# Column-group products of the modulation vectors, issued as groups of four

## The chip, the cores and the metric

One core of a Trainium2 chip runs the whole program as one launch. The time is device microseconds of that launch. Engines are named as in the profile: PE is TensorE (matrix products), PEld its weight loads, DVE is VectorE, ACT is ScalarE, POOL is GpSimd, SP is the queue from which nearly all DMAs are issued. Each engine works through its instructions in the order in which the scheduler of the language has put them; that order is fixed when the program is built.

## The reference

Two layers over 1024 latent and 256 context tokens of width 1024. In every layer six modulation vectors (shift, scale and gate of two sub-layers) are computed from the conditioning vector `c` and, for the context tokens, from `c_ctx`:

```python
c_act, cc_act = silu(c), silu(c_ctx)
for l in range(2):
    mx = c_act @ w_mod[l] + b_mod[l]        # 1024 x 6144, split into sh1, sc1, gt1, sh2, sc2, gt2
    mc = cc_act @ w_mod[l] + b_mod[l]
    hx = rmsnorm(x, g_pre_mix[l]) * (1 + sc1) + sh1
    yx, yc = ab_mixer(hx, hc, ...) if l == 0 else na_mixer(hx, hc, ...)
    x = x + gt1 * rmsnorm(yx, g_post_mix[l])
    fx = rmsnorm(x, g_pre_ffn[l]) * (1 + sc2) + sh2
    x = x + gt2 * rmsnorm(swiglu(fx, ...), g_post_ffn[l])
```

Layer 0's mixer is an RG-LRU block beside a 2-D Fourier transform, layer 1's is a neighbourhood attention; the context stream goes through the same sub-layers in layer 0.

## The kernel before, in words

The big matrix products split each float32 operand into two halves and take three products of 128 x 128 by 128 x 512 for one (`mm3`, lines 362 to 364). The modulation vectors are a different, thin sort of product: 2 rows (c and c_ctx, in `self.sil`, padded to 32 columns) against 1024 x 6144 float32 weights. One tile of weights is 128 rows by 512 columns, 256 KB, loaded to a buffer named `mraw`. Its product has an output of 32 x 512, and so four of them fit beside each other in one PSUM tile of 128 x 512: product j goes to partitions 32j to 32j+31 with `tile_position=(0, 32 * j)`, the j-th group of 32 columns of the array. [...] I call products that stand next to each other in PE's order, with no other work between, a **run**.

The vectors come in groups g of 2048 columns, and in three manners:

- Layer 0, g = 0, in quarters of 512 columns at the start of the program (`quarter` in `mixer`, lines 571 to 600). Step r of a quarter loads four tiles (rows 128k, k = 4r to 4r+3, line 583; a ring of 10 buffers) and issues their products (line 584); product j of a step takes row tile 4r + j. Quarter q+1 is issued between the first projections' products (`early_mm`).
- Layer 0, g = 1 and 2, in `mod_steps` (lines 419 to 435): 16 steps of four tiles (line 416) and four products (line 430), one for each column group j. The ring `mraw` has 3 buffers here (`open_mraw()`, line 670). `fill()` puts 12 of the steps between the LRU's parts, and the last four stand in the Fourier part (`for f in mods: f()`). The bias (line 478) and a gain (line 499) pass through the same ring.
- Layer 1, in `mod_steps_dve` (lines 437 to 474): DVE multiplies each tile by the column `sil[:, k, w]` and adds it up into `acc` (lines 452 and 454), and one product with a column of ones (line 460, `sum_up`) sums each `acc` over its partitions. g = 0 has two rows (c and c_ctx) and is done in layer 0's FFN, first half (`ffn_up`). g = 1 and 2 have one row, `acc` is a ring of 2, and they are fillers in the first block of `ffn_down`: after 8 loads of a column group j comes its sum. That block multiplies 22 tiles of hidden units by each half of w_down's columns; at the change of halves DVE takes the first half's sums from PSUM (`PostNorm.done`, line 257).

After the last product of a group `mod_row` adds the bias (DVE, line 480), and `mod_finish` turns the row into columns (PE, line 487).

Of the kernel before, what the change touches and what calls it, by code (L numbers as in the profile page):

```python
# [8 lines left out]
F32 = mybir.dt.float32  # L9
# [7 lines left out]
P = 128  # L17
# [4 lines left out]
KD = D // P  # L22
# [259 lines left out]
class Kernel:  # L282
# [130 lines left out]
    def mod_load(self, l, g, k, j):  # L413
# [2 lines left out]
        self.nc.sync.dma_start(out=raw, in_=self.a["w_mod"][l, k * P:(k + 1) * P, c:c + 512])  # L416
        return raw

    def mod_steps(self, l, g, pp, tag):

        nc = self.nc
        st = {}

        def step(k):
            if k == 0:
                st["ps"] = self.t(pp, [P, 512], F32, tag)
            ps = st["ps"]
            for j in range(4):
                raw = self.mod_load(l, g, k, j)
                nc.tensor.matmul(ps[32 * j:32 * j + 32, :], self.sil[:, k, :], raw, start=(k == 0), stop=(k == KD - 1),  # L430
                                 tile_position=(0, 32 * j))
            if k == KD - 1:
                self.mod_finish(l, g, self.mod_row(l, g, ps), pp, tag)

        return [lambda k=k: step(k) for k in range(KD)]

    def mod_steps_dve(self, l, g, pp, tag, rows):


        nc = self.nc  # L440
        st = {"acc": {}}

        def add_up(j, ks):
            for k in ks:
                raw = self.mod_load(l, g, k, j)
                for w in rows:
                    if k == 0:
                        st["acc"][j, w] = self.t(self.mraw, [P, 512], F32, "acc", bufs=2)
                    acc = st["acc"][j, w]
                    s = self.sil[:, k, w:w + 1]  # L450
                    if k == 0:
                        nc.vector.tensor_scalar(acc, raw, s, None, op0=ALU.mult)
                    else:
                        nc.vector.scalar_tensor_tensor(acc, raw, s, acc, op0=ALU.mult, op1=ALU.add)

        def sum_up(j):
            if j == 0:
                st["ps"] = self.t(pp, [P, 512], F32, tag)
            for w in rows:
                nc.tensor.matmul(st["ps"][32 * j:32 * j + 32, :], self.ones[:, w, :], st["acc"][j, w], start=(w == rows[0]),  # L460
                                 stop=(w == rows[-1]), tile_position=(0, 32 * j))

        def step(j, h):
            if h == 0 and j > 0:
                sum_up(j - 1)
            add_up(j, range(4 * h, 4 * h + 4))

        def last():
            sum_up(3)
            st["mr"] = self.mod_row(l, g, st["ps"])  # L470

        return ([lambda j=j, h=h: step(j, h) for j in range(4) for h in range(2)]
                + [last, lambda: self.mod_finish(l, g, st["mr"], pp, tag)])
# [63 lines left out]
    def mixer(self):  # L537
        nc, tc, a = self.nc, self.tc, self.a
# [31 lines left out]
        def quarter(q):  # L570

            st = {}

            def step(r):
                if r == 0:
                    st["ps"] = self.t(z0p, [P, 512], F32, "m", bufs=2)
                    b = st["b"] = self.t(self.mraw, [P, 512], F32, "mraw")
                    nc.sync.dma_start(out=b, in_=a["bmod0"][:, q, :])
                for j in range(4):
                    k = 4 * r + j  # L580
                    raw = self.t(mrp, [P, 512], F32, "mraw")
                    src = a["w_mod"][0, k * P:(k + 1) * P, 0:2048].rearrange("p (v c) -> p v c", v=2)
                    nc.sync.dma_start(out=raw.rearrange("p (v c) -> p v c", v=2), in_=src[:, :, 256 * q:256 * q + 256])
                    nc.tensor.matmul(st["ps"][32 * j:32 * j + 32, :], self.sil[:, k, :], raw, start=(r == 0), stop=(r == 1),
                                     tile_position=(0, 32 * j))

            def finish():
                mr = self.t(sp, [P, 512], F32, "mq")
                nc.vector.tensor_tensor(mr, st["ps"], st["b"], op=ALU.add)
                pt = self.t(tp, [P, 4, P], F32, "t")  # L590
                for i in range(4):
                    nc.tensor.matmul(pt[:, i, :], mr[:, i * P:(i + 1) * P], self.sel[:, :, 0:64], start=True, stop=True)
                src = pt.rearrange("p (v i) (w r) -> p v i w r", v=2, w=2)
                c = slice(2 * q, 2 * q + 2)
                for w in range(2):
                    nc.vector.tensor_copy(self.mt[0][:, 0:2, w, c], src[:, :, :, w, 0])
                    nc.vector.scalar_tensor_tensor(self.G[0][0][:, w, c], self.mt[0][:, 1, w, c], 1.0, self.gpre[:, 0, 0, c],
                                                   op0=ALU.add, op1=ALU.mult)

            return [lambda: step(0), lambda: step(1), finish]  # L600
# [66 lines left out]
        self.ystack = ExitStack()  # L667
        rxp = self.pool("rx", side="left", stack=self.ystack)
        xtp = self.pool("xt", bufs=4, side="left", stack=self.ystack)
        self.open_mraw()  # L670
        tstack = ExitStack()
        lp = self.pool("lru", bufs=2, side="left", stack=tstack)
        ep = self.pool("lrup", side="left", stack=tstack)
# [1384 lines left out]
```

## Time and profile before

| | us |
|---|---|
| three timed runs | 2745.85, 2751.33, 2755.67; median 2751.33 |
| profiled execution, its own time | 2753.36 |
| span of it, first to last instruction | 2751.6 |

The mean granted clock of PE over the span is 0.978 of full speed. The views used below are the page (busy times of the engines), windows (the same for stretches of the span, with PE's granted clock and the DMA engines' share), the timelines of single engines (start, length and name of instructions in order; "[1.81 <-DMA x]" is idle time just before and what ended it), and the lists of waits (who waited for whom: total us, times, longest). The start of the span is 0.

### The profile page before, as it was taken

Reading aid. Unit: us, or ns where it says so; the run is one execution under the profiler, and the core shown is the slowest. Engines: PE = TensorE matmul, PEld = TensorE weight load, DVE = VectorE, ACT = ScalarE, POOL = GpSimd, SP = SyncE. Lnnn points to the kernel's source line nnn. Section 1 sums busy time; section 2 is a strip of 40 time slices with the busy share of each in tenths; the row PEclk is TensorE's granted clock in tenths of the full one; section 3 lists DMA queues with packets and bytes.
Section 4 is the critical chain, followed back from the end, with each engine's and each line's share of the span. In section 5 each row is a group of like instructions: output and inputs, shape, how many; then the busy total and the mean of one; then the engine's idle time right before and its main releaser. Section 6 shows DMA issues by size and latency. Waiting matters only on the chain. (4 is left out here: it accounts for less than half of the span.)

```text
span 2751.6 us, 36277 instructions
## 1 busy us (share of the span) xinstructions
PE 2603.5 (95%) x12770; PEld 2120.1 (77%) x12770; DVE 1716.0 (62%) x2576; ACT 1257.5 (46%) x2245; POOL 990.2 (36%) x868
## 2 busy tenths in 40 slices
PE   7999999899999999999978999999997999999997
PEld 3677577688888887777866787899875888888786
DVE  3765275866543435666567655788677666656966
ACT  3676255422222323334553333899754333333443
POOL 1000013544343441002036333788536554542811
PEclk9999999899999999999998999999999999999999
DMA  7333463233222126876535545878541333235534
GB/s 246 107 113 124 127 205 139 73 104 102 89 70 73 65 72 219 303 235 241 192 122 181 179 172 177 198 185 190 145 148 54 103 112 115 87 109 179 208 100 145
DMA packets 187815, 399.59 MB, mean 145 GB/s; under 512 B 19697, under 2 KB 50033, under 8 KB 185586
## 3 DMA queue, kind: packets, MB, share of 16 engines
q1 hardware_dynamic: 187634, 397.28, 44.9%
q8 instruction: 101, 1.65, 0.3%
q14 instruction: 80, 0.66, 0.1%
HBM read 311.75 MB, written 85.46 MB: 144 GB/s over the span
## 5 line engine op out<-in xcount | busy, mean ns | idle before, releaser
L362 PE MATMUL d<-u,u 128*128 128x512 f32 x768 | 305.9, 401 | 20.1 <-ACT u L328 10.7
L363 PE MATMUL d<-u,u 128*128 128x512 f32 x768 | 306.5, 399 | 11.3 <-DVE u L329 11.2
L364 PE MATMUL d<-u,u 128*128 128x512 f32 x768 | 305.0, 397 | 0.1
L328 ACT ACTIVATE u<-r 128x512 fp32r<-128x512 f32 x249 | 154.8, 628 | 246.2 <-DVE u L329 53.8
L329 DVE TENSOR_TENSOR s<-r,s 128x512 fp32r<-128x512 f32 x208 | 166.2, 805 | 158.5 <-ACT s L328 157.6
L262 POOL TENSOR_TENSOR ss<-ss 128x1 f32<-128x1 f32 x36 | 12.8, 356 | 672.0 <-ACT junk L260 671.9
L363 PE MATMUL g<-u,s 128*128 128x512 f32 x624 | 245.4, 394 | 5.2 <-POOL u L174 4.3
L362 PE MATMUL g<-u,s 128*128 128x512 f32 x624 | 244.6, 393 | 3.7 <-ACT u L124 1.9
L329 DVE TENSOR_TENSOR u<-r,u 128x512 fp32r<-128x512 f32 x249 | 190.9, 773 | 87.1 <-ACT u L328 83.9
L364 PE MATMUL g<-u,s 128*128 128x512 f32 x624 | 244.6, 392 | 0.0
L328 ACT ACTIVATE s<-r 128x512 fp32r<-128x512 f32 x208 | 127.5, 629 | 247.6 <-PE g L364 149.8
L200 POOL TENSOR_TENSOR r<-rg,ru 128x512 f32<-128x512 f32 x52 | 73.1, 1405 | 406.2 <-DMA rg<-in_w_gu_dram 140.6
L362 PEld LDWEIGHTS d<-u,u 128*128 128x128 f32 x768 | 147.2, 192 | 62.8 <-ACT u L328 18.2
L363 PEld LDWEIGHTS d<-u,u 128*128 128x128 f32 x768 | 147.3, 192 | 44.7 <-DVE u L329 15.4
L1651 POOL TENSOR_TENSOR s<-s,sm 128x640 f32<-128x640 f32 (+1 forms) x128 | 151.0, 1200 | 59.3 <-DVE sm L1647 51.0
L364 PEld LDWEIGHTS d<-u,u 128*128 128x128 f32 x768 | 147.6, 192 | 32.0 <-DVE u L329 1.2
L362 PE MATMUL d<-u,ga 128*128 128x512 f32 x416 | 164.4, 395 | 2.6 <-ACT ga L328 2.5
L364 PE MATMUL d<-u,ga 128*128 128x512 f32 x416 | 163.3, 393 | 0.7 <-DVE ga L329 0.6
L363 PE MATMUL d<-u,ga 128*128 128x512 f32 x416 | 163.2, 392 | 0.0
L1183 POOL TENSOR_TENSOR ub<-ub,ua 128x512 f32<-128x512 f32 x44 | 72.4, 1645 | 205.0 <-DVE ua L1182 198.0
L363 PEld LDWEIGHTS g<-u,s 128*128 128x128 f32 x624 | 118.2, 190 | 30.8 <-POOL u L174 5.5
L362 PEld LDWEIGHTS g<-u,s 128*128 128x128 f32 x624 | 118.1, 189 | 30.1 <-ACT u L124 3.5
(445 smaller groups left out, 6972.2 us busy)
## 6 DMA issues: line engine op xcount, KB each, us to landing
mraw<-in_w_mod_dram SPq DMA_DIRECT2D x192, 256.0 KB, 3.8
rg<-in_w_gu_dram SPq DMA_DIRECT2D x44, 512.0 KB, 4.3
ru<-in_w_gu_dram SPq DMA_DIRECT2D x44, 512.0 KB, 3.8
r<-in_w_down_dram SPq DMA_DIRECT2D x88, 256.0 KB, 4.1
u<-hd SPq DMA_DIRECT2D x44, 512.0 KB, 5.2
x<-x SPq DMA_DIRECT2D x40, 512.0 KB, 4.9
qd<-qd SPq DMA_DIRECT2D x32, 512.0 KB, 10.6
r<-in_w_qkv_dram SPq DMA_DIRECT2D x52, 256.0 KB, 3.1
```

The source lines that it names most:

```text
L200: pool(rs[3], rg[:, h1], ru[:, h1], op=ALU.subtract)
L262: nc.gpsimd.tensor_tensor(st, ss[:, 0:1], ss[:, 1:2], op=ALU.add)
L328: i = nc.scalar.activation(hi, src, AF.Copy) if eng == "act" else nc.vector.tensor_copy(hi, src)
L329: j = nc.vector.tensor_tensor(lo, src, hi.bitcast(F32), op=ALU.subtract)
L362: nc.tensor.matmul(ps, lhs[0], rhs[0], start=start, stop=False)
L363: nc.tensor.matmul(ps, lhs[0], rhs[1], start=False, stop=False)
L364: nc.tensor.matmul(ps, lhs[1], rhs[0], start=False, stop=stop)
L1183: pool(ub, ub, ua, op=add)
L1651: pin(nc.gpsimd.tensor_tensor(s, s, sm.to_broadcast([P, nl + L]), op=ALU.mult))
```

## The change

1. A new helper `four` issues the four products of a step in one piece, j = 3 first, then 0, 1, 2, and pins them in PE's order (`keep_in_program_order`). `mod_steps` and the quarters use it; all four loads of a step are issued first.
2. In layer 1, for the groups with one row, the four sums over partitions are issued together by `four` after the fourth column group, and `acc` becomes a ring of 4.
3. The ring `mraw` of the mixer grows from 3 to 5 buffers.

```diff
--- before.py
+++ after.py
@@ -416,6 +416,13 @@
         self.nc.sync.dma_start(out=raw, in_=self.a["w_mod"][l, k * P:(k + 1) * P, c:c + 512])
         return raw
 
+    def four(self, ps, pairs, start, stop):
+
+        for j in (3, 0, 1, 2):
+            w, r = pairs[j]
+            self.tc.keep_in_program_order(self.nc.tensor.matmul(ps[32 * j:32 * j + 32, :], w, r, start=start, stop=stop,
+                                                                tile_position=(0, 32 * j)))
+
     def mod_steps(self, l, g, pp, tag):
 
         nc = self.nc
@@ -424,13 +431,9 @@
         def step(k):
             if k == 0:
                 st["ps"] = self.t(pp, [P, 512], F32, tag)
-            ps = st["ps"]
-            for j in range(4):
-                raw = self.mod_load(l, g, k, j)
-                nc.tensor.matmul(ps[32 * j:32 * j + 32, :], self.sil[:, k, :], raw, start=(k == 0), stop=(k == KD - 1),
-                                 tile_position=(0, 32 * j))
+            self.four(st["ps"], [(self.sil[:, k, :], self.mod_load(l, g, k, j)) for j in range(4)], k == 0, k == KD - 1)
             if k == KD - 1:
-                self.mod_finish(l, g, self.mod_row(l, g, ps), pp, tag)
+                self.mod_finish(l, g, self.mod_row(l, g, st["ps"]), pp, tag)
 
         return [lambda k=k: step(k) for k in range(KD)]
 
@@ -445,7 +448,7 @@
                 raw = self.mod_load(l, g, k, j)
                 for w in rows:
                     if k == 0:
-                        st["acc"][j, w] = self.t(self.mraw, [P, 512], F32, "acc", bufs=2)
+                        st["acc"][j, w] = self.t(self.mraw, [P, 512], F32, "acc", bufs=2 if len(rows) > 1 else 4)
                     acc = st["acc"][j, w]
                     s = self.sil[:, k, w:w + 1]
                     if k == 0:
@@ -456,6 +459,10 @@
         def sum_up(j):
             if j == 0:
                 st["ps"] = self.t(pp, [P, 512], F32, tag)
+            if len(rows) == 1:
+                if j == 3:
+                    self.four(st["ps"], [(self.ones[:, rows[0], :], st["acc"][i, rows[0]]) for i in range(4)], True, True)
+                return
             for w in rows:
                 nc.tensor.matmul(st["ps"][32 * j:32 * j + 32, :], self.ones[:, w, :], st["acc"][j, w], start=(w == rows[0]),
                                  stop=(w == rows[-1]), tile_position=(0, 32 * j))
@@ -576,13 +583,13 @@
                     st["ps"] = self.t(z0p, [P, 512], F32, "m", bufs=2)
                     b = st["b"] = self.t(self.mraw, [P, 512], F32, "mraw")
                     nc.sync.dma_start(out=b, in_=a["bmod0"][:, q, :])
-                for j in range(4):
-                    k = 4 * r + j
+                todo = []
+                for k in range(4 * r, 4 * r + 4):
                     raw = self.t(mrp, [P, 512], F32, "mraw")
                     src = a["w_mod"][0, k * P:(k + 1) * P, 0:2048].rearrange("p (v c) -> p v c", v=2)
                     nc.sync.dma_start(out=raw.rearrange("p (v c) -> p v c", v=2), in_=src[:, :, 256 * q:256 * q + 256])
-                    nc.tensor.matmul(st["ps"][32 * j:32 * j + 32, :], self.sil[:, k, :], raw, start=(r == 0), stop=(r == 1),
-                                     tile_position=(0, 32 * j))
+                    todo.append((self.sil[:, k, :], raw))
+                self.four(st["ps"], todo, r == 0, r == 1)
 
             def finish():
                 mr = self.t(sp, [P, 512], F32, "mq")
@@ -667,7 +674,7 @@
         self.ystack = ExitStack()
         rxp = self.pool("rx", side="left", stack=self.ystack)
         xtp = self.pool("xt", bufs=4, side="left", stack=self.ystack)
-        self.open_mraw()
+        self.open_mraw(5)
         tstack = ExitStack()
         lp = self.pool("lru", bufs=2, side="left", stack=tstack)
         ep = self.pool("lrup", side="left", stack=tstack)
```

In all, PE's order had 64 runs of such products and now has 29; every product is still there. By part, from and to: quarters 14 and 7; `mod_steps` 38 and 16; sums of layer 1's g = 0 four and 4; of g = 1 and 2 eight and 2. Outside of the places where these products stood, PE's order is the same row for row from the Fourier part's end on, but for the neighbourhood of the eight sums.

**PE, LRU part** (a step of `mod_steps` between the gates' products `z<-us,gw` and the projection `z<-h,ws`; `t` is the PSUM tile of the vectors, `mraw` the loaded weights). The three products that stood in a run, and the fourth:

```order
 L364 MATMUL z_1376<-us_256_1043,gw_1034 128x512
-L430 MATMUL t_865<-mraw_1390,sil_79 32x512
-L430 MATMUL t_865<-mraw_1393,sil_79 32x512
-L430 MATMUL t_865<-mraw_1396,sil_79 32x512
+L423 MATMUL t_865<-mraw_1396,sil_79 32x512
+L423 MATMUL t_865<-mraw_1390,sil_79 32x512
+L423 MATMUL t_865<-mraw_1392,sil_79 32x512
+L423 MATMUL t_865<-mraw_1394,sil_79 32x512
 L362 MATMUL z_1407<-h_0_44_149,ws_1404 128x256
 L363 MATMUL z_1407<-h_0_44_149,ws_1404 128x256
```

```order
 L363 MATMUL z_1408<-h_1_48_153,ws_1404 128x512
 L364 MATMUL z_1408<-h_1_48_153,ws_1404 128x512
-L430 MATMUL t_865<-mraw_1399,sil_79 32x512
 L362 MATMUL z_1409<-h_2_49_154,ws_1404 128x512
 L363 MATMUL z_1409<-h_2_49_154,ws_1404 128x512
```

The fourth product moved up over 15 products of the projection into the run of the other three, and the product whose tile is loaded last now stands first.

**SP, Fourier part** (`sx` and `cc_` are tables of the transform that go through another ring). Before:

```order
L416 DMA mraw_2332<-in_w_mod_dram 128x512
L866 DMA wr_2363<-in_sx_dram 128x2x512
L866 DMA wr_2367<-in_sx_dram 128x2x512
L416 DMA mraw_2467<-in_w_mod_dram 128x512
L416 DMA mraw_2470<-in_w_mod_dram 128x512
L416 DMA mraw_2473<-in_w_mod_dram 128x512
L873 DMA wr_2373<-in_cc__dram 128x2x256
L416 DMA mraw_2476<-in_w_mod_dram 128x512
```

and now:

```order
L416 DMA mraw_2467<-in_w_mod_dram 128x512
L884 DMA araw_2383<-in_altc_dram 128x2
L888 DMA rraw_2387<-in_altr_dram 1x512
L416 DMA mraw_2469<-in_w_mod_dram 128x512
L416 DMA mraw_2471<-in_w_mod_dram 128x512
L873 DMA wr_2363<-in_sx_dram 128x2x512
L873 DMA wr_2367<-in_sx_dram 128x2x512
L416 DMA mraw_2473<-in_w_mod_dram 128x512
```

The first load of a step (2467) now stands ahead of the step before it on PE; the next two follow that step's products, and the fourth stands behind two tables of 512 KB.

**PE, sums of layer 1's g = 1.** The first of the four single products, and the place of the last one, where now all four stand:

```order
 L363 MATMUL g_8612<-u_8664,u_8674 128x512
 L364 MATMUL g_8612<-u_8664,u_8674 128x512
-L460 MATMUL g_8769<-acc_8618,ones_71 32x512
 L362 MATMUL d_8562<-u_8709,u_8714 128x512
 L363 MATMUL d_8562<-u_8709,u_8714 128x512
```

```order
+L364 MATMUL g_8612<-u_9106,u_9116 128x512
+L423 MATMUL g_8769<-acc_9066,ones_71 32x512
+L423 MATMUL g_8769<-acc_8618,ones_71 32x512
+L423 MATMUL g_8769<-acc_8772,ones_71 32x512
+L423 MATMUL g_8769<-acc_8919,ones_71 32x512
+L362 MATMUL d_8562<-u_9151,u_9156 128x512
```

The first three of the four sums moved back by up to 216 products of `ffn_down` to the fourth's place.

## Rows read from the trace of the kernel before

**Rows 1.** Page, part 1: busy us (share of span) xinstructions by engine.
```profile
PE 2603.5 (95%) x12770; PEld 2120.1 (77%) x12770; DVE 1716.0 (62%) x2576; ACT 1257.5 (46%) x2245; POOL 990.2 (36%) x868
```

**Rows 2.** Windows: stretch, length, busy us of PE/PEld/DVE/ACT/POOL, clock, DMA share, GB/s.
```profile
0.00:65.00 65.00, 47.01 (x219) 23.32 (x220) 23.98 (x63) 22.77 (x37) 8.11 (x22) 0.97 0.78 260
65.00:345.00 280.00, 270.74 (x1270) 189.67 (x1271) 154.57 (x231) 159.15 (x227) 3.52 (x4) 0.99 0.35 116
1060.00:1240.00 180.00, 174.69 (x725) 135.02 (x724) 118.01 (x205) 68.06 (x141) 1.04 (x1) 0.97 0.81 272
```

**Rows 3.** Timeline of PE, one product alone (L460): start, us, instruction, xcount.
```profile
1214.09 0.39 PE L364 MATMUL g<-u,u 128*128 128x512 f32 x1
1214.41 1.05 PE L460 MATMUL g<-acc,ones 128*32 128x512 f32 x2
1215.38 0.50 PE L362 MATMUL d<-u,u 128*128 128x512 f32 x1
1215.72 0.39 PE L363 MATMUL d<-u,u 128*128 128x512 f32 x1
```

**Rows 4.** Timeline of PE, four products together (L584).
```profile
57.97 1.06 PE L584 MATMUL m<-mraw,sil 128*32 128x512 f32 x8
58.96 0.38 PE L362 MATMUL z<-h,w 128*128 128x256 f32 x1
```

**Rows 5.** Timeline of PEld (weight loads), the same four products.
```profile
57.97 0.16 PEld L584 LDWEIGHTS m<-mraw,sil 128*32 128x32 f32 x8 [0.36 <-DMA lam<-in_lam_dram]
```

**Rows 6.** Windows, 4 us before the LRU stretch.
```profile
84.00:88.00 4.00, 4.00 (x21) 2.47 (x19) 4.00 (x9) 1.49 (x4) 0.00 (x0) 1.00 0.00 0
```

**Rows 7.** Timeline of SP (queue), loads of the second quarter.
```profile
18.28 6.65 SPq L583 DMA_DIRECT2D mraw<-in_w_mod_dram  x8
```

**Rows 8.** The tile mraw, stretch 16 to 26 us, issue to landing.
```profile
DMA to landing us min/median/max: 5.9/6.9/7.0
```

**Rows 9.** Waits of PE, 62 to 345 us: total, times, longest.
```profile
PE t L430 <- DMA mraw<-in_w_mod_dram: 5.9, 7, 1.8
```

**Rows 10.** Timeline of PE around the longest of these waits.
```profile
200.71 0.39 PE L364 MATMUL z<-h,ws 128*128 128x512 f32 x1
202.91 1.05 PE L430 MATMUL t<-mraw,sil 128*32 128x512 f32 x2 [1.81 <-DMA mraw<-in_w_mod_dram]
203.89 0.61 PE L362 MATMUL z<-h,ws 128*128 128x512 f32 x1
```

**Rows 11.** Windows just after that wait.
```profile
204.00:206.00 2.00, 2.00 (x7) 1.70 (x8) 0.00 (x0) 1.98 (x3) 0.00 (x0) 0.53 0.50 174
206.00:208.00 2.00, 2.00 (x7) 1.52 (x7) 0.00 (x0) 1.99 (x2) 0.00 (x0) 0.61 0.04 16
```

**Rows 12.** Waits of ACT, 80 to 300 us.
```profile
ACT xt L710 <- PE z L364: 71.9, 20, 15.7
```

**Rows 13.** Timeline of PE, Fourier stretch: a waiting product, and the last.
```profile
308.57 1.70 PE L430 MATMUL t<-mraw,sil 128*32 128x512 f32 x4 [1.10 <-DMA mraw<-in_w_mod_dram]
339.55 1.05 PE L430 MATMUL t<-mraw,sil 128*32 128x512 f32 x2
```

**Rows 14.** Timeline of SP (queue), Fourier stretch.
```profile
301.39 0.94 SPq L866 DMA_DIRECT2D wr<-in_sx_dram  x2
302.43 3.09 SPq L416 DMA_DIRECT2D mraw<-in_w_mod_dram  x3
```

**Rows 15.** Timeline of PE, layer 1's vectors: a wait, and the change of halves.
```profile
1084.42 1.61 PE L460 MATMUL g<-acc,ones 128*32 128x512 f32 x2 [2.01 <-DVE acc L454]
1164.04 0.80 PE L362 MATMUL d<-u,u 128*128 128x512 f32 x1 [3.30 <-DVE y L257]
```

**Rows 16.** Timeline of DVE before that change of halves.
```profile
1163.30 1.28 DVE L257 TENSOR_TENSOR y<-d,gg 128x512 f32<-128x512 f32 x2
```

**Rows 17.** Windows of that stretch.
```profile
1084.00:1088.00 4.00, 3.58 (x7) 1.80 (x8) 3.23 (x7) 0.75 (x2) 0.00 (x0) 0.60 0.94 335
1140.00:1160.00 20.00, 20.00 (x92) 16.52 (x91) 12.83 (x27) 7.55 (x18) 0.00 (x0) 1.00 0.95 353
```

## The prediction, made before the changed kernel was run

> **What bounds the kernel now.** I read the page's busy times first: PE is busy for 95% of the span, the next engine for 62% [rows 1]. So PE's own time is what counts, unless a stage shows otherwise. The windows of the three stretches that the change touches say where it does [rows 2]. In the start (0 to 65 us) PE works 47.0 of 65 us and the DMA engines 0.78 of it: loads share the limit. In the mixer (65 to 345 us) PE works 270.7 of 280 us, and DVE and ACT have 155 and 159: PE is the limit. In layer 1's `ffn_down` (1060 to 1240 us) PE works 174.7 of 180 us, with the DMA engines at 0.81. Then the timelines, for the price of one run.
>
> **The price of a run.** Around a single product [rows 3], two steps of the ordinary products, from the start of L364 at 1214.09 to that of L363 at 1215.72, take 1.63 us. Without it two steps take 2 x 20.00/92 = 0.43 us (92 products fill a window without a gap [rows 17]). One run of one product thus costs 1.63 - 0.43 = 1.20 us. From the product's start to the next ordinary one it is 0.97 us. Where four stand together [rows 4] that distance is 58.96 - 57.97 = 0.99 us: the four run beside each other, and three more products cost 0.02 us in all. So what a product costs is its run, and the change takes away 64 - 29 = 35 runs: 35 x 1.20 = 42 us if PE is the limit at every one of them.
>
> A rule speaks for a smaller gain. The Trainium skill (TensorE: Matmul & The Clock Gate, section "Measured speedup vs the span model") gives 2.38 times, not 3, for three products side by side in column groups; by that three would take 3/2.38 = 1.26 of one, an estimate of 0.13 x 0.97 = 0.13 us for each further one, and 35 products joining others would give back 4.4 us. Rows 3 and 4 show 0.02 us for three, so the sum leaves it out.
>
> **Part by part**, against the profiled execution (2753.4 us, 2.0 above the median of the runs).
>
> *Quarters, 14 runs to 7.* All seven on PE's path give 7 x 1.20 = 8.4. The loads of a step are now issued ahead of its first product, so x loads behind them on SP's queue start later, and just before the LRU stretch DVE, not PE, is full (4.00 of 4 us [rows 6]). The second quarter's loads go out from 18.28 us, eight in 6.65 [rows 7], and land 5.9 to 7.0 us after issue [rows 8]; the fourth is issued at 18.28 + 3 x 0.83 = 20.8 and lands by 27.8, 2.5 us after the first: what a group waits longer than its first product did is bounded by that. I take 6 of 7 runs, 7.2; bounds 3.6 (half) and 8.4.
>
> *`mod_steps`, 38 runs to 16.* Twelve fewer in the LRU part (14.4) and ten fewer in the Fourier part (12.0): 26.4. ACT waits 71.9 us for PE's products in the LRU part [rows 12], so it can follow a faster PE.
>
> *Old waits for single loads.* PE waits 5.9 us in all for the fourth or another load of a step [rows 9]. After the longest, 1.81 us at 202.91 [rows 10], the granted clock is 0.53 and 0.61 for two windows of 2 us [rows 11], mostly the lower of its two levels (1.2 of 2.4 GHz), where it is about 1 over the stretch: (0.47 + 0.39) x 2 = 1.7 us more. With five buffers an LRU group has its loads early: groups stand up to 91 products, 20 us, apart in the new order, and a load takes 7.0. I take 5.9 + 1.7 = 7.6 as gone.
>
> *New waits.* In the Fourier part the groups stand only 17 to 31 products apart in the new order, 4 to 7 us. A group holds four of five buffers, so three of the next four loads go out only after it, the last behind two tables of 512 KB. Before, a load issued at or after 302.43 [rows 14] was used at 308.57, with PE waiting 1.10 for it [rows 13]: 6.1 us from issue to use. Against a spacing of 4 to 7 that makes waits of 0 to 2.5. Three groups have another close ahead; I take 2.5 for the second of the four, whose last load stands behind the tables, and 0.25 for each of the two after it. The last group also moves up, and its row's transposes stand 11 products (2.4 us) behind it, with DVE's addition of the bias to be done in between: 0.5. Together -3.5; bounds 0 and -9 (three waits of 2.5 and a clock fall of 1.7).
>
> *Layer 1's sums, eight runs to two.* Three of the six, in the second half's vectors, stand where PE runs without gaps: 3 x 1.20 = 3.6. The three in the first half also free a wait of 2.01 for `acc` (L454) at 1084.42 [rows 15] and a clock of 0.60 after it, 0.4 x 4 = 1.6 [rows 17]: 3.6 + 2.0 + 1.6 = 7.2. But at the change of halves PE waits 3.30 us for DVE's L257 [rows 15, 16], DVE stands behind accumulations of the loads, and the loads run at 353 GB/s with 0.95 of the DMA engines [rows 17]. If the loads set when DVE gets there, PE arrives earlier and waits longer. I take half, 3.6; bounds 0 and 7.2. Together 7.2; bounds 3.6 and 10.8.
>
> *At no cost:* `acc` as a ring of four (DVE need not wait for a sum before the next column group; DVE is not the limit), and two more `mraw` buffers (no load is added). The same bytes move.
>
> Sum: 7.2 + 26.4 + 7.6 - 3.5 + 7.2 = 44.9. 2753.4 - 44.9 = 2708.5 for the profiled execution, **2707** by the median.
>
> **Rivals.**
>
> *Part of it is taken up by others* (2728). Half of the quarters' gain (3.6), half of the LRU part's, because the scan between its gates and projections runs on DVE and ACT (7.2), the Fourier part with the old waits gone and the worst new ones (12.0 + 5.9 - 9.0 = 8.9), layer 1 with the loads as its limit (3.6): 23.3, so 2753.4 - 23.3 - 2.0 = 2728. For it: DVE full at 84 to 88 us, the share of 0.95. Against: ACT's 71.9 us of waiting for PE, and 155 us of DVE in 280.
>
> *Groups wait for their last load* (2769, slower). A group starts only when all four tiles are there, as the last loaded one stands first in it. If its loads are late each time, PE waits 2.5 us (the spread of four loads) and loses 1.7 us of clock behind it, 4.2 x 16 = 67 us in `mod_steps`, against 42 of runs and 7.6 of old waits gained: 2753.4 + 67 - 50 - 2.0 = 2769. It decides from 50/16 = 3.1 us per group. For it: SP's loads of the Fourier part stand close to their use. Against: 12 of the groups are in the LRU part, up to 20 us apart with loads of 7.0 us.
>
> *Weight loads in line* (2713). The Trainium skill (the same page, section "Part 3: Packing small matmuls — row/col tiling") lets weight loads overlap products under way only where the row group differs, and here all four use the same rows. As a mechanism of this kernel: the eight loads of a group stand ahead of its products on PE, where they were hidden for a product alone. The trace has the eight within 0.16 us [rows 5]; at that price for each of 35 products that join another it costs 35 x 0.16 = 5.6 us, or 2713. Against it: with three products' loads in line the 0.99 us of rows 4 would be longer than the 0.97 of rows 3 by more than 0.02.
>
> *No effect* (2751): PE's time is not the path, and each run saved comes back as a wait. Against it stands PE's 95%.
>
> **How the numbers follow.** Forecast 0.70; taken up in part 0.18; groups wait 0.04; weight loads in line 0.04; no effect 0.04. The forecast's own range: 44.9 with the lower bounds of quarters and layer 1 and worst waits is 44.9 - 3.6 - 3.6 - 5.5 = 32.2, or 2719; with the upper bounds 44.9 + 1.2 + 3.6 + 3.5 = 53.2, or 2698; with 1 to 3 us for the scatter of the runs 2697 to 2722. The range takes in the second case, 2728, too: 2697 to 2729. A difference of 0.3%, 8 us, is about what a measurement of this kernel can tell from none. Faster by more: 0.70 + 0.18 + 0.04 = 0.92; within: 0.04; slower: 0.04.
>
> **What would show it.** The product line shows groups of four in about 1.06 us, one step apart from ordinary products by about 1 us, and 16 of them between 65 and 345 us. The mixer's stretch is about 30 us shorter, the start some 7, layer 1's some 7. PE waits for `mraw` before two or three groups of the Fourier part and hardly anywhere in the LRU part. The gap at layer 1's change of halves is longer than 3.30 if the loads set it, and if it is not, that term is 7.2. The forecast is wrong if groups take clearly over 1.06 us, if PE's busy time falls by 40 us while waits of its own grow by as much, or if groups of the LRU part wait for their loads.

## The result, and the profile after

Four runs of the changed kernel gave 2719.55 to 2730.56 us, median 2721.82, against 2750.7 for the kernel before: ratio 0.9901 (95% interval 0.9872 to 0.9929), 29 us faster. Two later comparisons of the same two kernels gave 0.9914 (0.9896 to 0.9933) and 0.9904 (0.9887 to 0.9921): 24 and 26 us. The profiled execution took 2720.2 us. The forecast was 2707, a gain of 44: right in its direction and inside its range, but the gain is about 0.6 of it.

The page's busy times after the change, which answer to [rows 1]:

```profile
PE 2558.7 (94%) x12770; PEld 2118.3 (78%) x12770; DVE 1713.7 (63%) x2576; ACT 1256.6 (46%) x2245; POOL 990.3 (36%) x868
```

PE has lost 44.8 us of busy time (35 runs of 1.20 us are 42), while the execution became only 33.2 us shorter: waits took a part back. That 44.8 comes so close to 42 is in part luck. A product at a lower clock counts as longer busy (43 products are 9.3 us in a window at 0.83 below, 32 are 9.9 in one at 0.50), and five profiles of the changed kernel and of near copies of it (the first, and after_again, after_third, pool_order and gap_fill below) lie between 2558.7 and 2571.0 us. The windows of the same three stretches, as far as their work now reaches (columns as in [rows 2]), and PE's timeline around two groups of the LRU part, answering to [rows 3, 4]:

```profile
0.00:65.00 65.00, 39.83 (x223) 25.36 (x224) 27.99 (x77) 25.25 (x40) 11.80 (x25) 0.98 0.78 260
65.00:321.00 256.00, 248.13 (x1286) 189.07 (x1285) 152.49 (x222) 160.17 (x230) 0.00 (x0) 0.98 0.39 129
1032.00:1210.00 178.00, 171.59 (x745) 139.34 (x745) 119.70 (x215) 69.31 (x145) 0.00 (x0) 0.96 0.83 276
```

```profile
112.21 1.06 PE L423 MATMUL t<-mraw,sil 128*32 128x512 f32 x8
113.21 0.38 PE L362 MATMUL z<-h,ws 128*128 128x256 f32 x1
130.78 1.07 PE L423 MATMUL t<-mraw,sil 128*32 128x512 f32 x8
```

One product is two instructions in the trace, so x8 are the four. A group of four costs 0.99 to 1.00 us from its start to the next product, as the quarter's group did before. All LRU groups look like this. The same two steps in the kernel before (three products together; the fourth, 15 products later, was a run of its own):

```profile
117.50 1.06 PE L430 MATMUL t<-mraw,sil 128*32 128x512 f32 x6
137.23 1.06 PE L430 MATMUL t<-mraw,sil 128*32 128x512 f32 x6
```

With the same 90 other products between and no wait, the step took 19.73 us and takes 18.57 now. The run that went was worth 1.16 us, against 1.20 in the forecast.

The list of waits of PE from 62 to 321 us shows what is left, and what is new (total, times, longest); the 5.9 us in seven waits of [rows 9] have become one:

```profile
PE z L362 <- DVE h L540: 2.7, 1, 2.7
PE z L362 <- ACT us L328: 2.6, 1, 2.6
PE t L423 <- DMA mraw<-in_w_mod_dram: 2.5, 1, 2.5
PE z L897 <- DVE ab L329: 1.4, 1, 1.4
PE z L929 <- ACT cc L328: 0.8, 1, 0.8
```

The first stands at the end of the start, the last three at the head of the Fourier part. The second, at 89 us, stands where PE waited 1.8 us for another tile (DVE's `xt`) before.

To see where time went I cut PE's timeline at landmarks that both kernels have: the first product of the gates (`z<-us,gw`), the first transposition of the Fourier part (`z<-ident,xt`), the first product of the output projection (`d<-u,u`), and in `ffn_down` its first product and the end of PE's first wait for DVE's L266. One column has the stages of three profiles in which that stage's code is the old one (the kernel before, and two of the experiments below), the other those of three profiles of the changed kernel:

| stage, us | old code | changed | mean gain | forecast |
|---|---|---|---|---|
| start | 88.1, 87.9, 87.8 | 85.5, 85.6, 85.8 | 2.3 | 7.2 |
| LRU part | 212.8, 211.7, 210.4 | 194.1, 192.8, 194.1 | 18.0 | 14.4 + 4.1 + 1.7 = 20.2 |
| Fourier part | 48.7, 48.4, 48.3 | 41.4, 42.3, 43.4 | 6.1 | 12.0 + 1.8 - 3.5 = 10.3 |
| layer 1's sums | 202.6, 198.1, 197.9 | 196.5, 196.3, 193.1 | 4.2 | 7.2 |
| sum | | | 30.6 | 44.9 |

(Of the old waits of 5.9 us, 1.8 stood in the Fourier part [rows 13] and 4.1 in the LRU part.) Stages that the change does not touch differ among profiles of one kernel by some us too; layer 1's attention took 261.0 to 264.7 us in these three. Three profiles are few, then. Many of the experiments below have the changed code in one stage or another; with all of these the gains are 2.7 (start, eight profiles), 17.6 (LRU part, six), 4.8 (Fourier part, six) and 3.0 (layer 1's sums, ten), 28.1 together.

**Start.** Two things took back a part of the gain. The first is POOL's order. Timelines of POOL and DVE, and the product that waited on PE:

```profile
59.01 1.65 POOL L696 TENSOR_TENSOR q<-e,q 128x8 f32<-128x8 f32 x1 [1.41 <-DVE q L695]
61.05 0.56 POOL L371 TENSOR_TENSOR rstd<-rstd,mhalf 128x1 f32<-128x1 f32 x1
```

```profile
61.65 0.75 DVE L529 TENSOR_SCALAR x<-x,rstd 128x1024 f32<-128x1024 f32 x1 [0.78 <-POOL rstd L371]
62.31 0.29 DVE L540 CAST h<-hf 128x256 fp32r<-128x256 f32 x1
```

```profile
62.66 0.58 PE L362 MATMUL z<-h,w 128*128 128x256 f32 x1 [2.71 <-DVE h L540]
```

In the kernel before:

```profile
67.22 0.60 POOL L371 TENSOR_TENSOR rstd<-rstd,mhalf 128x1 f32<-128x1 f32 x1
69.09 2.08 POOL L689 TENSOR_TENSOR q<-e,q 128x8 f32<-128x8 f32 x1 [1.28 <-DVE q L688]
```

The scheduler has put the power for the LRU's decay (L696, POOL) ahead of the last token tile's rstd; in the kernel before it stood behind it (L689). The tile is scaled late, DVE's casts of h (L540) queue behind it, and PE waits 2.71 us. The diff touches none of these instructions of POOL and DVE.

The second stands at the head of the start. PE's first transpositions and its first product of 128x512, before and then now:

```profile
23.98 1.16 PE L592 MATMUL t<-sel,mq 128*128 128x128 f32 x8 [0.79 <-DVE mq L589]
29.65 0.50 PE L362 MATMUL z<-h,w 128*128 128x512 f32 x1
```

```profile
24.19 2.08 PE L599 MATMUL t<-sel,mq 128*128 128x128 f32 x8 [0.89 <-DVE mq L596]
32.61 0.50 PE L362 MATMUL z<-h,w 128*128 128x512 f32 x1
```

The first quarter ends at nearly the same time, as PE waits for its loads in both. But the same eight transpositions behind it take 2.08 us in place of 1.16, and the product at 29.65 comes at 32.61. Eight profiles have the quarters as groups and POOL's order as it is here. In all of them the transpositions take 2.08 us, and that product comes at 31.0 to 33.8 us; in the three with the old quarters it comes at 29.4 to 29.7. From this product to the LRU part it is 58.5 us with the old quarters and 52.3 to 53.1 now: the runs are saved there, less the wait for h. What slows PE is not shown. The clock column reads 1.00 from 24 to 32 us in both kernels; what differs ahead of it is that PE, whose first group waits for four loads, was busy for 3.87 us from 12 to 24 us, and for 7.66 before.

**Fourier part.** PE's waits at its head, SP's queue there, and windows (columns as before):

```profile
283.49 0.63 PE L897 MATMUL z<-ident,xt 128*128 128x128 f32 x4 [1.39 <-DVE ab L329]
288.51 1.07 PE L423 MATMUL t<-mraw,sil 128*32 128x512 f32 x8 [2.45 <-DMA mraw<-in_w_mod_dram]
292.37 0.39 PE L929 MATMUL z<-cc,abc 128*128 128x256 f32 x1 [0.78 <-ACT cc L328]
```

```profile
279.67 0.83 SPq L416 DMA_DIRECT2D mraw<-in_w_mod_dram  x2
280.59 0.90 SPq L873 DMA_DIRECT2D wr<-in_sx_dram  x2
281.54 0.93 SPq L416 DMA_DIRECT2D mraw<-in_w_mod_dram  x2
```

```profile
284.00:288.00 4.00, 2.06 (x12) 1.38 (x9) 0.80 (x3) 1.49 (x4) 0.00 (x0) 1.00 0.80 291
294.00:298.00 4.00, 4.00 (x17) 2.86 (x20) 1.73 (x4) 1.21 (x3) 0.00 (x0) 0.60 0.39 145
```

After the group at 278.59 everything is asked for at once: 1 MB of tables with the vectors' loads on either side, at 291 GB/s. The last load of the group at 288.51 stands behind the tables, is issued near 282 and is there at 288.5. PE is busy half of the time from 284 to 288 us, and from 294 to 298 its clock is 0.60. In the kernel before, the windows from 280 to 345 us all had a clock of 1.00.

**Layer 1.** PE's gap at the change of halves, which answers to [rows 15], and what DVE waited for ahead of it:

```profile
1131.67 0.80 PE L362 MATMUL d<-u,u 128*128 128x512 f32 x1 [5.99 <-DVE y L257]
```

```profile
1116.44 0.75 DVE L457 SCALAR_TENSOR_TENSOR acc<-mraw,sil,acc 128x512 f32<-128x512 f32 x1 [5.70 <-DMA mraw<-in_w_mod_dram]
1121.12 0.75 DVE L457 SCALAR_TENSOR_TENSOR acc<-mraw,sil,acc 128x512 f32<-128x512 f32 x1 [2.39 <-DMA mraw<-in_w_mod_dram]
1130.93 1.28 DVE L257 TENSOR_TENSOR y<-d,gg 128x512 f32<-128x512 f32 x2
```

PE comes to the change of halves earlier and waits 5.99 us in place of 3.30.

### The profile page after: what moved, and what is told of

Its sections match the earlier page's. It is cut to its first block, busy times and chain, and to the rows that moved or that the text cites. A ratio compares the mean times of both kernels' runs of the same rounds, so it can differ in the third digit from the quotient of the medians.

```text
span 2718.4 us, 36271 instructions
## 1 busy us (share of the span) xinstructions
PE 2558.7 (94%) x12770; PEld 2118.3 (78%) x12770; DVE 1713.7 (63%) x2576; ACT 1256.6 (46%) x2245; POOL 990.3 (36%) x868
## 5 line engine op out<-in xcount | busy, mean ns | idle before, releaser
L363 PEld LDWEIGHTS g<-u,s 128*128 128x128 f32 x624 | 118.2, 189 | 30.5 <-POOL u L174 6.5
```

Source lines behind the costliest of these rows:

```text
L363: nc.tensor.matmul(ps, lhs[0], rhs[1], start=False, stop=False)
```

## The experiments

**Each part alone.** `mod_only` keeps `four` and the five buffers in `mod_steps` alone, `quarters_only` keeps it in the quarters alone, `sums_only` in layer 1's sums alone; the other parts are as before the change. For the first, as a difference from the changed kernel:

```diff
-                self.four(st["ps"], todo, r == 0, r == 1)
+                    nc.tensor.matmul(st["ps"][32 * j:32 * j + 32, :], self.sil[:, k, :], raw, start=(r == 0), stop=(r == 1),
+                                     tile_position=(0, 32 * j))
...
-            if len(rows) == 1:
-                if j == 3:
-                    self.four(st["ps"], [(self.ones[:, rows[0], :], st["acc"][i, rows[0]]) for i in range(4)], True, True)
-                return
```

> Layer 0's 16 steps of mod_steps as groups of four with five buffers; quarters and layer 1's sums as before. Theory (a run costs 1.20 us wherever PE is the limit, whatever its number of products): 22 runs fewer, 26.4 us, plus most of the old waits of 7.6, less what the Fourier part gives back. In the trace of the changed kernel the stretch from 85 to 345 us gained 25 us net; so 24 to 28 us faster than before (about 2724 against 2750), with PE waiting 2 to 3 us for the last load of the first Fourier group. Rival (the gain is that of the buffers alone, the old waits): 6 to 8 us faster. Rival (the whole term of the forecast, 30.5): Fourier part without the new waits.

Measured: 0.9919 (0.9894 to 0.9945), 22 us faster; theory's 24 to 28 lie inside the interval. The buffers alone (6 to 8 us) are out; so is the whole term of 30.5. The LRU part took 192.9 us, the Fourier part 43.8, with this wait of PE at its head:

```profile
289.69 1.07 PE L423 MATMUL t<-mraw,sil 128*32 128x512 f32 x8 [2.56 <-DMA mraw<-in_w_mod_dram]
```

> The quarters alone as groups of four; everything else as before. Theory: seven runs fewer, 7 x 1.20 = 8.4 us by the end of the quarters at most; in the trace of the changed kernel 4 to 5 us had been gained there and some 3 us were left when the LRU part begins, because the last quarter's token tiles are normalised late (POOL works on the decay's power ahead of the last rstd). So 2 to 5 us faster, with PE waiting 2 to 3 us for DVE's h of the last token tile near 62 us. Forecast on record: 7.2. Rival (the loads set the start, 0.78 of the DMA engines): no change, 0 to 1 us.

Measured: 0.9988 (0.9975 to 1.0001), 3.3 us faster with an interval that reaches no change. The LRU part begins at 84.8 us in place of 88. The wait is there in the same length, so it comes with the quarters' part of the change alone:

```profile
62.06 0.49 PE L362 MATMUL z<-h,w 128*128 128x256 f32 x1 [2.71 <-DVE h L540]
```

> Layer 1's sums over partitions for g = 1 and 2 as groups of four, with four acc buffers; everything else as before. Theory: six runs fewer (7.2) and the wait of 2.0 for acc with its clock fall of 1.6 gone, but the three runs of the first half given back at the change of halves, where the gap before PE grows from 3.3 to about 6: net 6 us faster (5 to 8). Rival (no loads at their limit; gap stays 3.3): 9 to 11 us faster. Rival (sums off the path): 0.

Measured: 0.9974 (0.9961 to 0.9987), 7 us faster (4 to 11). The gap at the change of halves is longer, as theory had it:

```profile
1159.91 0.80 PE L362 MATMUL d<-u,u 128*128 128x512 f32 x1 [6.67 <-DVE y L257]
```

By the profiles the gain is smaller: both halves took 196.7 us (193.1 to 198.2 in ten profiles with the gathered sums), against 198.1 and 197.9 in two profiles with the old sums (quarters_only, mod_only) and 202.6 in the kernel before. In those two the gap was 2.5 and 1.0 us, and the granted clock in the 16 us around its end 1.00, where the kernel before had 0.79. Which of 1 to 6 us is the rule stays open. The three parts add up to 33 us, the whole gave 24 to 29; the intervals allow that.

**What does a group cost?**

```diff
-        for j in (3, 0, 1, 2):
+        for j in (3, 0, 1, 2) if start or not one else (3,):
...
-            self.four(st["ps"], [(self.sil[:, k, :], self.mod_load(l, g, k, j)) for j in range(4)], k == 0, k == KD - 1)
+            self.four(st["ps"], [(self.sil[:, k, :], self.mod_load(l, g, k, j)) for j in range(4)], k == 0, k == KD - 1, k < KD - 1)
```

> The changed kernel, but in 14 of the 16 groups of mod_steps only product j = 3 is done; the other 42 products of layer 0's g = 1 and 2 are left out (their tiles are still loaded). Theory (what a group costs is its run, the four products stand side by side): from the start of a single product to the next ordinary one 0.97 to 0.99 us as for a group of four, so 42 x 0.007 = 0.3 us, no difference that can be told from the changed kernel (2720 to 2723). Rival (each further product of a group costs 0.13 us): 42 x 0.13 = 5.5 us faster than the changed kernel. Rival (weight loads of a group in line, 0.11 us for each of 84): 9 us faster.

By this edit 12 of the 16 groups lose three products, 36 in all, not 14 and 42 as the expectation says: the last step of g = 1 and of g = 2 keeps its four as well. PE's timeline in the LRU part:

```profile
127.59 1.05 PE L423 MATMUL t<-mraw,sil 128*32 128x512 f32 x2
128.57 0.38 PE L362 MATMUL z<-h,ws 128*128 128x256 f32 x1
```

A single product costs 0.98 us to the next one, a group of four 0.99 to 1.00. From one step to the next, with 90 other products between, it is 18.53 to 18.56 us here in five steps, and in the changed kernel 18.57 or 18.58 in three of them and 18.82 or 18.83 in two, where the products just behind the group come later; why is not shown. Three further products thus take 0.01 to 0.04 us, in two steps 0.27, and 0.12 on average, against 1.16 for a run. The price is that of the run.

By the figure of the Trainium skill (TensorE: Matmul & The Clock Gate, section "Measured speedup vs the span model"), 2.38 times for three in column groups, three side by side would take 1.26 of one, an estimate. This trace stays below it: by that estimate the three further products of a group cost some 0.4 us, and here they cost 0.27 at most.

The kernel took 2714.8 us, 0.9872 (0.9839 to 0.9905), more than theory had said. Most of the difference lies in the Fourier part: 36.1 us there, not 41 to 46. The tiles that no product reads are free as soon as they are asked for, so the next loads go out early; three steps' single products stand in one run, and only one wait for `mraw` is left:

```profile
283.15 2.76 PE L423 MATMUL t<-mraw,sil 128*32 128x512 f32 x6
285.84 2.32 PE L927 MATMUL z<-cx,ab 128*128 128x512 f32 x9
288.50 1.06 PE L423 MATMUL t<-mraw,sil 128*32 128x512 f32 x8 [0.34 <-DMA mraw<-in_w_mod_dram]
```

Against 48.5 that is 12.4 us less, where the forecast had 12.0 for the runs and 1.8 for the old waits. Some 0.7 us of it come from having two runs in place of four: these take 2.69 and 1.00 us to the next product and, by the forecast's 1.20 - 0.97, about 0.2 each around it, 4.1 in place of 4 x 1.20 = 4.8. The rest says what the Fourier part could give with its loads in time. The run at 283.15 shows a limit of the rule, too: its three products all stand on column group j = 3, and take 2.69 us to the next product, not 1.00. So what is nearly free beside another product is one on a different column group.

**The start.**

```diff
-        nc.gpsimd.tensor_tensor(q1, e8, q1, op=ALU.pow)
+        with tc.issue_after(self.rpow.ins):
+            nc.gpsimd.tensor_tensor(q1, e8, q1, op=ALU.pow)
```

(`rpow` is the last rstd's instruction.)

> The changed kernel, but POOL's power for the LRU's decay is queued behind the last rstd of the tokens. Theory (the changed kernel's start gives back 2.7 us at 62.7 us because POOL does that power, which waits 1.4 us for DVE, ahead of the last rstd): PE's wait of 2.71 for DVE's h shrinks to under 0.5, and PE is 2 to 3 us ahead of the changed kernel at 80 us. Rival (the last token tile is late by its load, not by POOL): wait unchanged, no gain. Rival (the scan's first inputs are what counts): gained at 65 us, given back in the wait for ACT's us near 89 us, which grows from 2.6 to about 5.

The wait is gone, and PE is 2.9 to 3.1 us ahead of the first profile of the changed kernel from 85 to 270 us; the wait for ACT's us near 86 us is 2.76, where the changed kernel had 2.61:

```profile
60.35 0.39 PE L362 MATMUL z<-h,w 128*128 128x256 f32 x1 [0.26 <-DVE h L540]
```

Two more kernels with this edit (spread5 and tables5 below) have no such wait either. From the first product of 128x512 to the LRU part the three take 49.1 to 50.1 us, against 52.3 to 53.1 without the edit. So POOL's order took some 3 us of the quarters' gain. The one execution took 2729.3 us all the same. At the end of the Fourier part, behind whose wait its clock fell lower (below), it is 0.5 us behind the first profile, and it loses 8.6 more in later stages, whose code is the same; that was not traced.

**Fewer buffers.** `ring4` has `self.open_mraw(4)`.

> The changed kernel with 4 mraw buffers in the mixer in place of 5, so that no load of a group can go out before the group ahead of it is done. Theory (waits only where groups stand 4 to 9 us apart): LRU groups, 18.5 us apart, wait no longer than with 5 buffers; the Fourier part's waits for mraw grow from 2.5 to 4 to 10 us in all. Rival (the loads of a whole group are late everywhere, the slower rival of the forecast): PE waits for mraw before most LRU groups too, 1 to 3 us each, 15 us or more in all.

PE's list of waits from 62 to 325 us:

```profile
PE t L423 <- DMA mraw<-in_w_mod_dram: 3.5, 3, 2.9
```

3.5 us in three waits, and of that only 0.2 in the LRU part; theory had 4 to 10. The first profile with five buffers had 2.5, but the two later ones (after_again, after_third) had 3.5 and 3.8, so no worth of the fifth buffer is seen here. Groups that wait for their last load everywhere, the slower rival, are out.

**All groups ahead of the Fourier part.** (`lru16` has six buffers besides.)

```diff
         for j in range(4):
+            fill()
             fourier_in(j)
```

> The changed kernel, but all 16 groups of layer 0's mod_steps stand in the LRU part and the projections ahead of the Fourier part (a second fill in each of the four last projections), and the ring has 6 buffers. Theory (the Fourier part of the changed kernel loses some 5 us to late loads and to the clock behind them, since its groups stand 4 to 9 us apart): the Fourier part has no wait for mraw, the four groups cost the same 1.2 us each where they stand now, and the end of the mixer's projections and transform comes 4 to 6 us earlier than in the changed kernel. Rival (the four groups only bring their waits along, because the second group of a pair stands as close behind the first): PE waits for mraw at up to four places near 240 to 290 us, no gain or a loss up to 5 us.

The rival holds. Three groups wait for `mraw` (3.8 us), and the Fourier part without any group still took 40.5 us, since DVE's splits of the transposed tiles are now waited for:

```profile
PE z L898 <- DVE ab L329: 3.4, 1, 3.4
PE z L901 <- DVE ab L329: 2.5, 1, 2.5
```

LRU and Fourier part took 243.1 us together, against 235.1 to 237.5 in the three profiles of the changed kernel (up to 240.4 in others with the same code there). The groups had filled holes. So had the single products before: this one, in the old Fourier part, stood where PE now waits 1.39 us for `ab`:

```profile
304.12 1.04 PE L430 MATMUL t<-mraw,sil 128*32 128x512 f32 x2 [0.70 <-DMA mraw<-in_w_mod_dram]
```

**Layer 1's loads moved.** `gap_fill` has `mods[10:20] + [lambda: None] * 2 + mods[20:]` as fillers.

> The changed kernel, but in layer 1's vectors two filler places are left empty between g = 1 and g = 2, so that g = 2's loads begin after the change of halves. Theory (loads at their limit hold DVE up there: it waits 5.7 us for one tile, and PE's gap of 6.0 follows): the gap shrinks to 1 to 4 us, and the stretch from 1060 to 1300 us is 2 to 5 us shorter. Rival (DVE's own work, not the loads, sets the gap): the gap stays at 5 to 6 us.

The gap did not shrink:

```profile
1140.34 0.79 PE L362 MATMUL d<-u,u 128*128 128x512 f32 x1 [7.04 <-DVE y L257]
```

```profile
1130.41 0.49 DVE L455 TENSOR_SCALAR acc<-mraw,sil 128x512 f32<-128x512 f32 x1 [6.28 <-DMA mraw<-in_w_mod_dram]
```

By these lines DVE still waits for a load ahead of its L257, one that now goes out at 1121.86, with the tiles of x of the next stage just ahead of it. So the edit did not do what the expectation wanted: g = 2's first load still goes out ahead of the change of halves, where PE waits until 1140.34. That the loads hold DVE up is seen in each profile; that moving them helps is not shown.

**Better order in the Fourier part.** `spread5` has the edit of pool_order, and gives out the four groups between the transform's blocks:

```diff
-        for f in mods:
-            f()
...
+            fill((1, 1, 2, 0)[j])
```

> The changed kernel with two edits: POOL's power for the decay behind the last rstd, and the last four groups of mod_steps given out between the blocks of the transform, so that they stand 27 to 45 products apart in place of 17 to 31. Theory (late loads near 285 us and the clock behind them are what the Fourier part loses; the start loses 2.9 us to POOL's order): no wait for mraw over 0.5 us from 280 us on, granted clock 0.9 or more from 290 to 300 us, and 5 to 9 us faster than the changed kernel (about 2712 to 2717). Rival (the tables' splits on DVE and ACT bound the head of the Fourier part, and the group only filled the hole): PE waits there for cc or ab in place of mraw, 2 to 3 us, and only the start's 2.9 us are left. Rival (the vectors come too late for the output projection): a new wait of PE after 320 us for the group's row, 1 to 4 us, nothing gained.

Measured: 0.9892 (0.9872 to 0.9911) beside 0.9914 for the changed kernel on the same chip, 2715.3 against 2724.3 us; the intervals overlap. No wait for `mraw` is left, but the first rival is there, and the Fourier part took 46.3 us in the profiled execution:

```profile
PE z L928 <- ACT cc L328: 2.9, 1, 2.9
PE z L926 <- ACT er L328: 1.7, 1, 1.7
```

`tables5` adds that the small table `cc` is loaded and split first, the large `sx` later (`table` is the loading code of the tables as a function):

```diff
-        for nm in ("cx", "sx"):
...
+        table("cx")
+        table("cc_")
...
+        table("sx")
+        table("sc_")
```

> The kernel spread5 with one more edit: the small table cc is loaded and split ahead of the two large tables sx (1 MB), which in the two kernels before stood ahead of cc and of two loads of the vectors on the queue, and whose split on ACT stood ahead of those of the transposed tiles. Theory (the head of the Fourier part is bound by what is loaded there, 2 MB between 280 and 288 us, in the order of the queue; whatever stands last is waited for): PE's waits for er and cc (1.7 + 0.8 + 2.9 us in spread5) shrink to under 2 us together, no wait for mraw over 0.5, the Fourier part takes 38 to 41 us (48.5 before the change, 41.4 and 42.3 in the two profiles of the changed kernel, 46.3 in spread5, 36.1 with three products of four left out), and the kernel is 8 to 13 us faster than the changed one. Rival (DVE's and ACT's splits themselves bound the head): the Fourier part stays at 44 to 46 us. Rival (the order only moves the wait to sx): a wait for sx of 2 us or more near 305 us.

The waits for er and cc are gone and another stands in their place, so neither theory nor the named rivals hold:

```profile
PE z L907 <- DVE abc L329: 3.8, 1, 3.8
```

The Fourier part took 43.0 us, and the kernel 0.9897 (0.9878 to 0.9916), 2717.9 us, beside 2718.1 for the changed kernel: no difference. In the four orders seen (the changed kernel's, lru16, spread5, tables5) PE stands still for about 4.6 to 6.8 us at this head, each time for another of loads, ACT's and DVE's splits. No version clearly beats the changed kernel.

**The changed kernel again.**

> The changed kernel once more, on the same chip as the next one. Theory (its gain is 28 to 33 us; in the Fourier part PE stands still for 4 to 5 us near 285 us and the granted clock behind that differs from one execution to the next): 27 to 33 us faster than before; in the profile 290 to 300 us the granted clock is between 0.50 and 0.83, the stretch from 280 us to the end of the transform up to 4 us longer than in the first profile. Rival (the first profile shows all there is): the same clock of 0.83 again, and the forecast's 44 only missed by waits.

> The changed kernel a third time, beside tables5 on the same chip. Theory: 23 to 29 us faster than before, as in the two comparisons so far; Fourier part 41 to 46 us by the clock behind its wait near 285 us; the start's wait of 2.7 us for DVE's h there again. Rival (the first comparison was right, 29 or more).

0.9914 and 0.9904. The first is less than theory's 27 to 33 us, and its clock behind the Fourier wait was 0.83, as in the first profile and as its rival said; the second lies in theory's 23 to 29. The group near 288 us waited 2.65 and 2.22 us, and the start's wait was there both times. Over more profiles the clock behind the Fourier wait varies. The same window in after_again, after_third, pool_order and gap_fill, whose code is the same there (pool_order is 3 us further on in it):

```profile
290.00:300.00 10.00, 9.32 (x43) 6.32 (x43) 4.26 (x12) 3.40 (x10) 0.00 (x0) 0.83 0.51 163
```

```profile
290.00:300.00 10.00, 10.00 (x44) 6.53 (x41) 5.20 (x15) 3.34 (x9) 0.00 (x0) 0.73 0.49 158
```

```profile
290.00:300.00 10.00, 10.00 (x37) 7.09 (x37) 2.78 (x8) 2.43 (x7) 0.00 (x0) 0.56 0.29 93
```

```profile
290.00:300.00 10.00, 9.93 (x32) 6.35 (x33) 5.74 (x16) 3.26 (x9) 0.00 (x0) 0.50 0.50 161
```

0.83 costs 1.7 us in ten, 0.50 costs 5. In the last two a neighbouring window is low as well: 0.76 from 280 us on in pool_order, 0.84 from 300 us on in gap_fill. One more profile with the same code there, mod_only, has 0.54. The Fourier part took 42.3, 43.4, 44.9 and 46.2 us in these four, in the order of the clock.

## Why the prediction was right, and where it was wrong

- *What bounds the kernel, and the price of a run.* Right. A step of the LRU part with the same other products became 1.16 us shorter for the run that went, against 1.20, and a group costs nearly as little as a single product (one_of_four). PE's busy time fell by 44.8 us, against 42 for 35 runs, a weaker witness, as it scatters by 12 us.
- *LRU part.* Right within the spread of the profiles: 18.0 of 20.2.
- *Quarters, "I take 6 of 7 runs, 7.2".* The price was right, the net was mis-sized: 2.3 by the stages, 3.3 (0 to 7) by quarters_only. From the first product of 128x512 on, the changed kernel is 5.4 to 6.2 us shorter up to the LRU part, and 8.4 to 9.4 with POOL's order put right; seven runs are 8.4. What was lost is the order of POOL with DVE's work behind it, some 3 us, and 1.4 to 4.4 us of slow products behind the first quarter. I looked for the loss in the second quarter's loads [rows 7, 8], where no group waits. POOL's order is the scheduler's and changed with the products' places; pool_order shows it. The order of all engines in the changed program could have been read ahead of the forecast: the power stands ahead of the last rstd in it.
- *New waits in the Fourier part, "Together -3.5".* The sign and the cause were right, size and place were not. The first of the four groups has the long wait, not the second, since it is the first group's last load that stands behind the tables. Together with the hole that a single product used to fill (1.39) and cc (0.78) it is 4.6 us of waiting in the first profile, and 1.7 to 5 us of clock behind it, more where a second window is low. The bound of -9 held that, for the wrong rows: I counted waits of 2.5 three times and the clock once.
- *Layer 1, "I take half".* The mechanism was right (gap 5.4 to 6.8 us in place of 3.3). The sum of 7.2 is 4.2 by the three profiles of the table, 3.0 by all and 7 (4 to 11) by sums_only's times. It is less by the stages because the profile of the kernel before had a lower clock and a longer gap there than two other profiles with the old sums. I took one execution's wait and clock as the rule.
- *Rivals.* "Part of it is taken up by others" (2728) describes three of the four stages, though not the LRU part. The measured 2722 is nearer to it than to 2707, and stands at the upper end of the forecast's own range (2697 to 2722), which was then stretched to 2729 to take this rival in. So the time fell into the range with about half of three terms missing. Weight loads in line and groups that wait everywhere are out; "no effect" as well.
- The stages give 30.6 us by three profiles and 28.1 by all, and 24 to 29 are timed. What is left between them is no more than stages with unchanged code differ by among profiles of one kernel; it was not traced further.

## What to carry to other kernels

Thin products on different column groups cost by the run, not by the piece: here 1.16 to 1.20 us for each place at which PE turned from wide products to thin ones and back, and 0.12 us on average for the second to fourth together. Three on one column group cost 2.69 us. Gathering them pays where their data is early; where a group comes close behind another, it trades many small holes, which single products fill, for one long wait with a lower clock behind it. Moving products on one engine moves the scheduler's order on others: compare all engines' orders, and read prices of waits and clock from more than one execution.

## What the runs showed of the hardware

Nearly the same wait (2.2 to 3.0 us, with PE 57 to 69% busy from 280 to 290 us) goes with a granted clock of 0.83, 0.73, 0.56 or 0.50 from 290 to 300 us. I had expected a fixed fall, as after the 1.81 us wait of [rows 10, 11]. With one and the same code the Fourier part takes 41.4 to 46.2 us.
